# A two-layer S5, Conformer and pooling backbone: modulation in fewer VectorE instructions, x read by place in chunk, and copies moved to ScalarE

## The chip, the core and the metric

The kernel runs on one core of a Trainium2 chip. The metric is the device time of one execution in microseconds (us), the median over runs. The engines in the text are TensorE (PE in the rows), VectorE (DVE), ScalarE (ACT), GpSimd (POOL) and the queue that issues the transfers (SP).

## What is computed

The input is 512 latent tokens of 1024 features and a context of 256 tokens. Two layers follow each other. Layer 0 mixes the tokens with two heads side by side, 32 groups of a bidirectional state-space model and a convolution over 31 tokens; layer 1 takes centred means over windows of 2 to 16 tokens. Both end in an MLP with a squared ReLU. Each norm is followed by a scale and a shift from a projection of c:

```python
n_x = modulate(rms_norm(h, norm_mix_g[i]), sh1, sc1)      # h * (1 + scale) + shift
# layer 0
z = h @ w_in                                              # u | v | gt, 512 each
ya = y_f + flip(y_b) + d_skip * u                         # state-space model, both directions, skip term
ya = gelu(ya);  ya = ya * sigmoid(ya @ w_glu)
vb = silu(layer_norm(conv(v * sigmoid(gt)) + conv_b))
y = concatenate([ya, vb]) @ w_out
# every layer
h = h + g1 * y
h = h + g2 * (relu(modulate(rms_norm(h), sh2, sc2) @ w1) ** 2) @ w2
```

## The kernel before

Features lie on the 128 partitions, in 8 tiles; tokens lie along a row. Matmuls keep fp32 accuracy with three products: each operand is split into a high part, rounded to the fast format fp32r, and the rest, the low part (`split`, L143: a conversion and a subtraction). `mm3` (L147) issues the three products. The matmul operands of a whole stage are the tiles `nh` and `nl`. Weights arrive raw, ScalarE makes the high part and VectorE the low one (`Ring.get`, L223).

**u stage** (`mixer0`, L292, up to about 90 us). The latent x is loaded into `x0` (`load_x`, L239), the position table is added (`add_pos`, L243), and the square root of the mean square is spread to all partitions as R. For each of 8 feature tiles, `u_mod` (L423) multiplies x by R on VectorE, applies scale and shift on ScalarE, and splits the result on VectorE. That ScalarE instruction also changes the order of the tokens: the state-space model cuts the row into chunks of T = 8 tokens, and the matmuls want the tokens by their place k in the chunk, so it reads with a step of 8 elements:

```python
S.activation(t2.rearrange("p (k c) -> p k c", k=T), t.rearrange("p (c k) -> p k c", k=T),
             AF.Identity, bias=ab[:, d, 0, v:v + 1], scale=ab[:, d, 1, v:v + 1])
split(oh, ol, t2, V, el)
```

The same is done for the context (`c_step`, L447), with operands `c`. The products u are collected in six banks, `ux` and `uc`. Sixteen copies, VectorE and ScalarE in turn (`ENG`, key z), bring them into Z; TensorE turns Z over in eight groups of four, and two copies a group, one on each engine, fill U (after L880).

**Steps.** The 32 groups go through the state-space model in 8 steps of four. `step_params` (L581) makes a step's matrices, three steps ahead of `step_main` (L661), where the scan runs on VectorE. One of these matrices, Kt, holds the first taps of the model; its diagonal block has the skip term d_skip. It is put together in `stage` (from L646): for each group two ScalarE copies out of PSUM, a multiply-add of the identity with d_skip, an add of the backward taps; then eight DMAs spread it over the partitions. Between the steps stand the value projections (`vgt`), the convolutions (`conv`) and modulation matmuls, by a list (`FILL`).

**Norm, gelu, gate** (297 to about 320 us). `conv_norm` (L782) makes the conv half of the operands, `nh[4..7]`. `y_out` (L722) turns the model's output over and applies gelu in a scratch tile `ge`; its split fills `nh[0..3]`. `glu_gate` (L824) multiplies with the gate: it adds the high and the low part up again into `yg`, multiplies, and splits once more. Then `out_proj` (L280) runs, first the conv half.

**MLPs and pooling** (from about 345 us). `mlp_norm` (L274) normalises one half of the tokens: VectorE multiplies by R (`norm_mod`, L262), ScalarE applies scale and shift, VectorE converts the high part and subtracts for the low one. `pool_half` (L1072) uses the same `norm_mod`. `up` and `down` stream the weights, three matmuls each.

No order is written by hand: the framework places every instruction by a simulated timeline, so a change in one place moves instructions elsewhere.

Of the kernel before, what the change touches and what calls it, by code (L numbers as in the profile page):

```python
# [17 lines left out]
L = 512  # L18
# [26 lines left out]
    wg="VVVV", gl="VVVV", yl="VVVV", ge="S", z="VS", ul="VVVVVVVV", ucl="VVVVVVVV", pos="VVVVVVVV", ph="V", bb="V", eb="V",  # L45
# [52 lines left out]
def body(tc, I, out, dbg=None):  # L98
# [53 lines left out]
    with tc.tile_pool(name="persist", bufs=1) as P, tc.tile_pool(name="ps", bufs=1, space=PSUM) as PS:  # L152
# [86 lines left out]
        def load_x(t):  # L239
            for d0 in range(0, KT, 2):  # L240
                dma(t[:, d0:d0 + 2], I["xT"][:, d0:d0 + 2])

        def add_pos(e, t, d):  # L243
            hv = t[:, d].rearrange("p (r c) -> p r c", r=8)
            pe = posr[:, d, :, None] if d < 4 else posc[:, d - 4, None, :]
            add(e, hv, hv, pe.to_broadcast([128, 8, 64]))

# [14 lines left out]
        def norm_mod(h, tk, a, b, e):  # L262
            n = tk.stop - tk.start
            R = bcast_rsqrt(sumsq(h, tk), n, D)
            if "G" in ENG[e]:
                rb = tmp("rb", n)
                copy(S, rb, R)
            for d in range(KT):
                t = tmp("tn", n)
                x = E(e, d)  # L270
                mul(x, t, h[:, d, tk], rb if x is G else R)
                yield d, t, a(d), b(d)

        def mlp_norm(h, l, tk):  # L274
            for d, t, a, b in norm_mod(h, tk, lambda d: mod[:, l, 4, d:d + 1], lambda d: mod[:, l, 3, d:d + 1], "tn"):
                S.activation(t, t, AF.Identity, bias=b, scale=a)
                split(nh[:, d, tk], nl[:, d, tk], t, E("nc", d), E("nl", d))
# [14 lines left out]
        def mixer0(P0):  # L292
# [8 lines left out]
            dsk = P0.tile([PH, NG], F32, name="dsk")  # L301
            S2 = P0.tile([128, KT, 32], F32, name="S2")
# [13 lines left out]
            load_x(x0)  # L316
# [53 lines left out]
            def norm_x():  # L370
                for d in range(KT):
                    add_pos(E("pos", d), x0, d)
# [50 lines left out]
            def u_mod(src, R, n, d, v, oh, ol, el):  # L423
                t = tmp("tn", n)
                mul(V, t, src, R)
                t2 = tmp("tm", n)
                S.activation(t2.rearrange("p (k c) -> p k c", k=T), t.rearrange("p (c k) -> p k c", k=T),
                             AF.Identity, bias=ab[:, d, 0, v:v + 1], scale=ab[:, d, 1, v:v + 1])
                split(oh, ol, t2, V, el)
# [128 lines left out]
            def discretise_b(cfr, cfi):  # L558
                def bc(ap):
# [21 lines left out]
            def step_params(st):  # L581
# [67 lines left out]
                for qq in range(GQ):  # L649
# [3 lines left out]
                    q = GQ * st + qq  # L653
                    stt(stage[:, qq, n:n + PH], ident[0:PH, 0:PH], dsk[:, q:q + 1], stage[:, qq, n:n + PH], OP.mult, OP.add)
                    add(V, stage[:, qq, n:n + PH], stage[:, qq, n:n + PH], kb[r, n:n + PH])
# [599 lines left out]
```

## Time and profile before

| | us |
|---|---|
| median of 3 runs | 1141.48 |
| lowest, highest | 1140.08, 1145.19 |
| the profiled execution, time | 1145.11 |
| the profiled execution, span | 1143.3 |
| TensorE busy | 1052.2 (92%) |
| VectorE busy | 843.8 (74%) |
| ScalarE busy | 510.9 (45%) |

The times count from the start of the span. A line `L139` or `L116` is a helper's, so that the names of the tiles tell the place. "Busy" is a share over stages that are bound in different ways; the stretches have to be read one by one.

### The profile page before, as it was taken

How to read it: one execution, taken by the hardware profiler on the slowest of the kernel's cores; microseconds unless marked ns; L12 is line 12 of the kernel's file. 1: busy time of each engine (PE TensorE's matmuls, PEld its weight loads, DVE VectorE, ACT ScalarE, POOL GpSimd, SP SyncE). 2: the span in 40 equal slices, each digit the busy share in tenths (PEclk: the TensorE clock that was granted, in tenths of full speed). 3: DMA queues.
4: the chain of work that ended last, by engine and by line, in shares of the span. 5: the costliest groups of instructions: out<-in, count | busy, mean ns of one | idle time of the engine just before them, and what ended most of it. 6: DMA issues, size and time to landing. Idle time of an engine off the chain costs nothing.

```text
span 1143.3 us, 19141 instructions
## 1 busy us (share of the span) xinstructions
PE 1052.2 (92%) x7342; PEld 894.6 (78%) x7342; DVE 843.8 (74%) x1745; ACT 510.9 (45%) x894; POOL 26.2 (2%) x46
## 2 busy tenths in 40 slices
PE   4888998884898989999999999989979999999996
PEld 3566564543588988888789999989979988888896
DVE  8994988898789789877755669989976543343365
ACT  4553452453545653322324456567545433133153
POOL 1002000000000000000000000000000000000000
PEclk9999998986799999999999999989989999999998
DMA  9442543236245678878754555545536633323352
GB/s 359 133 129 73 160 123 86 65 87 227 68 130 189 194 252 297 289 259 258 255 182 149 178 180 184 167 124 171 168 109 185 186 106 96 92 92 100 103 167 92
DMA packets 63596, 184.84 MB, mean 162 GB/s; under 512 B 8464, under 2 KB 14608, under 8 KB 63376
## 3 DMA queue, kind: packets, MB, share of 16 engines
q1 hardware_dynamic: 63504, 183.61, 50.3%
q8 instruction: 58, 0.95, 0.3%
q14 instruction: 34, 0.28, 0.1%
HBM read 174.96 MB, written 2.10 MB: 155 GB/s over the span
## 4 chain that ended last, share of the span: by engine, by line
PE 52%; DMA 8%; DVE 6%; issue 1%; ACT 1%; POOLq 0%; POOL 0%; DVEq 0%; ACTq 0%
PE ps L148 17%; PE ps L150 17%; PE ps L149 16%; DMA wraw<-in_wadaT 5%; DMA wraw<-in_w 3%; DVE junk L988 2%; DVE wlo L116 2%; ACT whi L139 1%; DVE tn L110 1%; PE ps_r L194 0%; PE ps_p L148 0%; PE ps_p L149 0%; PE ps_p L150 0%; DVE rl L110 0%; PE ps_ms L187 0%
## 5 line engine op out<-in xcount | busy, mean ns | idle before, releaser
L139 ACT ACTIVATE whi<-wraw 128x1024 fp32r<-128x1024 f32 (+1 forms) x232 | 231.5, 1000 | 409.4 <-PE ps L149 267.0
L116 DVE TENSOR_TENSOR wlo<-wraw,whi 128x1024 fp32r<-128x1024 f32 (+1 forms) x232 | 266.2, 1149 | 112.1 <-ACT whi L139 108.4
L148 PE MATMUL ps<-nh,whi 128*128 128x256 f32 (+3 forms) x768 | 248.2, 325 | 10.2 <-DVE nh L141 5.2
L150 PE MATMUL ps<-nh,wlo 128*128 128x256 f32 (+3 forms) x768 | 247.3, 323 | 2.4 <-DVE wlo L116 2.4
L149 PE MATMUL ps<-nl,whi 128*128 128x256 f32 (+3 forms) x768 | 247.4, 323 | 0.0
L150 PE MATMUL ps<-hh,wlo 128*128 128x512 f32 (+3 forms) x768 | 244.1, 318 | 0.4 <-DVE wlo L116 0.4
L148 PE MATMUL ps<-hh,whi 128*128 128x512 f32 (+3 forms) x768 | 243.9, 318 | 0.0
L149 PE MATMUL ps<-hl,whi 128*128 128x512 f32 (+3 forms) x768 | 243.2, 317 | 0.0
L148 PEld LDWEIGHTS ps<-nh,whi 128*128 128x128 f32 x768 | 149.3, 195 | 21.9 <-DVE nh L141 6.3
L150 PEld LDWEIGHTS ps<-nh,wlo 128*128 128x128 f32 x768 | 149.0, 194 | 13.8 <-DVE wlo L116 3.8
L149 PEld LDWEIGHTS ps<-nl,whi 128*128 128x128 f32 x768 | 149.0, 194 | 10.2
L150 PEld LDWEIGHTS ps<-hh,wlo 128*128 128x128 f32 x768 | 144.3, 188 | 12.1 <-DVE wlo L116 1.3
L149 PEld LDWEIGHTS ps<-hl,whi 128*128 128x128 f32 x768 | 144.3, 188 | 10.9
L148 PEld LDWEIGHTS ps<-hh,whi 128*128 128x128 f32 x768 | 144.5, 188 | 9.8
L125 DVE SCALAR_TENSOR_TENSOR h<-ps,mod,h 128x512 f32<-128x512 f32 (+3 forms) x96 | 54.9, 572 | 86.9 <-PE ps L150 86.5
L988 DVE SCALAR_TENSOR_TENSOR junk<-wraw,csil 128x1024 f32<-128x1024 f32 x56 | 68.3, 1220 | 20.4 <-DMA wraw<-in_wadaT 20.3
L116 DVE TENSOR_TENSOR hl<-rl,hh 128x256 fp32r<-128x256 f32 (+3 forms) x96 | 48.4, 511 | 4.8 <-ACT hh L139 3.7
L1014 ACT ACTIVATE rl<-ps 128x256 f32<-128x256 f32 (+3 forms) x96 | 42.0, 437 | 3.4 <-PE ps L149 2.1
L148 PE MATMUL ps_o<-nh,whi 128*128 128x256 f32 x128 | 37.7, 299 | 5.2 <-DVE nh L141 2.7
L149 PE MATMUL ps_o<-nl,whi 128*128 128x256 f32 x128 | 37.5, 294 | 2.5 <-DVE nl L116 2.5
L150 PE MATMUL ps_o<-nh,wlo 128*128 128x256 f32 x128 | 37.4, 298 | 2.1 <-DVE wlo L116 1.9
L348 PE MATMUL ps_ada<-wraw,S 128*32 128x128 f32 x512 | 28.1, 317 | 5.7 <-DMA wraw<-in_wada0b 5.5
(279 smaller groups left out, 1437.1 us busy)
## 6 DMA issues: line engine op xcount, KB each, us to landing
wraw<-in_w SPq DMA_DIRECT2D x192, 512.0 KB, 3.6
wraw<-in_wadaT SPq DMA_DIRECT2D x56, 512.0 KB, 4.6
wraw<-in_wada0b SPq DMA_DIRECT2D x24, 512.0 KB, 4.1
wraw<-in_wout SPq DMA_DIRECT2D x32, 256.0 KB, 2.8
cvt<-vpad SPq DMA_DIRECT2D x64, 67.5 KB, 2.0
wah<-in_wada SPq DMA_DIRECT2D x16, 256.0 KB, 4.6
wraw<-in_wada SPq DMA_DIRECT2D x8, 512.0 KB, 5.3
wraw<-in_win_vg SPq DMA_DIRECT2D x8, 512.0 KB, 4.0
```

The lines of the kernel that those rows point to most:

```text
L110: e.tensor_tensor(o, a, b, op=OP.mult)
L116: e.tensor_tensor(o, a, b, op=OP.subtract)
L125: V.scalar_tensor_tensor(o, a, s, b, op0=op0, op1=op1)
L139: S.activation(o, a, AF.Copy)
L148: PE.matmul(ps, wh, xh, start=first, stop=False)
L149: PE.matmul(ps, wh, xl, start=False, stop=False)
L150: PE.matmul(ps, wl, xh, start=False, stop=last)
L348: PE.matmul(ps[32 * j:32 * j + 32, i * 128:i * 128 + 128], S2[:, kt, :], w[kt], start=kt % 2 == 0, stop=kt % 2 == 1, tile_position=(0, 32 ...
L988: V.scalar_tensor_tensor(junk, w, 1.0, csil, op0=OP.mult, op1=OP.mult, accum_out=r)
L1014: S.activation(t, ps, AF.Relu)
```

## The change

The modulation gets shorter: VectorE multiplies by the scale and by R in one instruction, ScalarE adds the shift and writes the high part directly, and VectorE makes the low part from the same product (`split_shift`); the conversion goes. To do so in the u stage, x and the context come already ordered by place in chunk (xK, ctxT), and the position table is added in that order (`add_pos_k`); the latent stream h is still loaded from xT later. The skip term of a step is one add of a prepared table Dd, behind the four adds of the backward taps. All copies into Z and U run on ScalarE, and so do the high parts of the gelu, the norm and the gate. The gelu output is kept in four tiles of its own, so that the gate needs no adding up. The smaller DMA scratch leaves room in SBUF. What is computed stays.

```diff
@@ ENG
-    ... z="VS", ...
+    ... z="S", ...
@@ body
-        def load_x(t):
+        def load_x(t, src):
             for d0 in range(0, KT, 2):
-                dma(t[:, d0:d0 + 2], I["xT"][:, d0:d0 + 2])
+                dma(t[:, d0:d0 + 2], I[src][:, d0:d0 + 2])
+        def add_pos_k(e, t, d):
+            hv = t[:, d].rearrange("p (k r m) -> p k r m", k=T, r=8)
+            if d < 4:
+                pe = posr[:, d, None, :, None]
+            else:
+                pe = posc[:, d - 4].rearrange("p (m k) -> p k m", k=T)[:, :, None, :]
+            add(e, hv, hv, pe.to_broadcast([128, T, 8, 8]))
-        def norm_mod(h, tk, a, b, e):
+        def norm_scale(h, tk, a, b):
             n = tk.stop - tk.start
             R = bcast_rsqrt(sumsq(h, tk), n, D)
...
             for d in range(KT):
                 t = tmp("tn", n)
-                x = E(e, d)
-                mul(x, t, h[:, d, tk], rb if x is G else R)
-                yield d, t, a(d), b(d)
+                stt(t, h[:, d, tk], a(d), R, OP.mult, OP.mult)
+                yield d, t, b(d)
+        def split_shift(o_h, o_l, t, b):
+            S.activation(o_h, t, AF.Identity, bias=b)
+            stt(o_l, t, b, f(o_h), OP.add, OP.subtract)
         def mlp_norm(h, l, tk):
-            for d, t, a, b in norm_mod(...):
-                S.activation(t, t, AF.Identity, bias=b, scale=a)
-                split(nh[:, d, tk], nl[:, d, tk], t, E("nc", d), E("nl", d))
+            for d, t, b in norm_scale(...):
+                split_shift(nh[:, d, tk], nl[:, d, tk], t, b)
@@ mixer0
+            Dd = P0.tile([PH, NG, PH], F32, name="Dd")
-            load_x(x0)
+            load_x(x0, "xK")
-                    add_pos(E("pos", d), x0, d)
+                    add_pos_k(E("pos", d), x0, d)
@@ u_mod
                 t = tmp("tn", n)
-                mul(V, t, src, R)
-                t2 = tmp("tm", n)
-                S.activation(t2.rearrange("p (k c) -> p k c", k=T), t.rearrange("p (c k) -> p k c", k=T),
-                             AF.Identity, bias=ab[:, d, 0, v:v + 1], scale=ab[:, d, 1, v:v + 1])
-                split(oh, ol, t2, V, el)
+                stt(t, src, ab[:, d, 1, v:v + 1], R, OP.mult, OP.mult)
+                split_shift(oh, ol, t, ab[:, d, 0, v:v + 1])
@@ discretise_b
+                mul(V, Dd, ident[0:PH, None, 0:PH].to_broadcast([PH, NG, PH]), dsk[:, :, None].to_broadcast([PH, NG, PH]))
@@ step_params, for each of the four groups of a step, and after them
-                    q = GQ * st + qq
-                    stt(stage[:, qq, n:n + PH], ident[0:PH, 0:PH], dsk[:, q:q + 1], stage[:, qq, n:n + PH], OP.mult, OP.add)
                     add(V, stage[:, qq, n:n + PH], stage[:, qq, n:n + PH], kb[r, n:n + PH])
+                add(V, stage[:, :, n:n + PH], stage[:, :, n:n + PH], Dd[:, qs])
@@ y_out
-                    t = tmp("ge")
+                    t = P0.tile([128, 512], F32, name="ge", tag="ge", bufs=4)
+                    ges.append(t)
...
-                    split(nh[:, b], nl[:, b], t, V, E("yl", b))
+                    split(nh[:, b], nl[:, b], t, S, E("yl", b))
@@ conv_norm
-                    split(nh[:, 4 + j], nl[:, 4 + j], xn, V, V)
+                    split(nh[:, 4 + j], nl[:, 4 + j], xn, S, V)
@@ glu_gate
-                    y = tmp("yg")
-                    add(V, y, f(nh[:, j]), f(nl[:, j]))
+                    y = ges[j]
                     mul(V, y, y, glu[j])
-                    split(nh[:, j], nl[:, j], y, V, E("gl", j))
+                    split(nh[:, j], nl[:, j], y, S, E("gl", j))
@@ the transposes into U
                 copy(S, us[:, :, NCC:128], pv)
-                copy(V, us[:, :, 0:NCC], pv[:, :, NCH:NJ])
+                copy(S, us[:, :, 0:NCC], pv[:, :, NCH:NJ])
@@ pool_half
-                    S.activation(xp[:, 16 + 16 * x:16 + 16 * x + ns], t, AF.Identity, bias=b, scale=a)
+                    S.activation(xp[:, 16 + 16 * x:16 + 16 * x + ns], t, AF.Identity, bias=b)
@@ layout, kernel
-    X["ctxT"] = a["ctx"][0].T.reshape(KT, 128, LC).transpose(1, 0, 2)
+    X["xK"] = X["xT"].reshape(128, KT, NCH, T).transpose(0, 1, 3, 2).reshape(128, KT, L)
+    X["ctxT"] = a["ctx"][0].T.reshape(KT, 128, NCC, T).transpose(1, 0, 3, 2).reshape(128, KT, LC)
-    nc = _bacc.Bacc("TRN2", target_bir_lowering=False, num_devices=1)
+    nc = _bacc.Bacc("TRN2", target_bir_lowering=False, num_devices=1, dynamic_dma_scratch_size=2048)
```

The order on three places follows. First ScalarE at the end of the u stage (`tm` and `nh` are the modulated tiles of x, `c_...` those of the context, `uc` and `ux` the banks of products that Z is copied from). Before:

```order
L427 ACTIVATE tm<-tn,ab 128x512
L139 ACTIVATE hx<-Cc 64x4x16
L636 ACTIVATE hx<-Cc 64x4x16
L139 ACTIVATE hx<-Cc 64x4x16
L636 ACTIVATE hx<-Cc 64x4x16
L633 ACTIVATE Oi<-Oi 128x4x128
L139 ACTIVATE Z<-uc 32x32x16 x2
L139 ACTIVATE stage<-ps_k 16x112
L139 ACTIVATE Z<-uc 32x32x16
L139 ACTIVATE Z<-ux 64x32x16 x2
L139 ACTIVATE Z<-uc 32x32x16
L139 ACTIVATE Z<-ux 64x32x16 x2
```

and now:

```order
L282 ACTIVATE c_839<-tn,ab 128x256
L282 ACTIVATE nh<-tn,ab 128x512
L139 ACTIVATE hx<-Cc 64x4x16
L646 ACTIVATE hx<-Cc 64x4x16
L139 ACTIVATE hx<-Cc 64x4x16
L646 ACTIVATE hx<-Cc 64x4x16
L643 ACTIVATE Oi<-Oi 128x4x128
L139 ACTIVATE Z<-uc 32x32x16 x8
L139 ACTIVATE Z<-ux 64x32x16 x8
L139 ACTIVATE stage<-ps_k 16x112
L769 ACTIVATE sg<-ps_vg 128x512
L139 ACTIVATE U<-ps_u 128x4x96
```

The sixteen copies into Z stand in one row behind each other, all of uc first, and the `stage` copy that stood among them is behind. On TensorE the same place, the last products of the context (`uc`) and of x (`ux`), was before:

```order
L435 MATMUL uc<-wuh,c_865 128x512
L436 MATMUL uc<-wul,c_865 128x512
L437 MATMUL uc<-wuh,c_865 128x512 x2
L435 MATMUL ux<-wuh,nh 128x512
L436 MATMUL ux<-wul,nh 128x512
L435 MATMUL ux<-wuh,nh 128x512
L436 MATMUL ux<-wul,nh 128x512
L435 MATMUL ux<-wuh,nh 128x512
```

and is now:

```order
L443 MATMUL ux<-wuh,nh 128x512
L444 MATMUL ux<-wul,nh 128x512
L443 MATMUL ux<-wuh,nh 128x512
L444 MATMUL ux<-wul,nh 128x512
L443 MATMUL ux<-wuh,nh 128x512
L444 MATMUL ux<-wul,nh 128x512
L653 MATMUL ps_k<-Or,Bb 16x128
L445 MATMUL uc<-wuh,c_839 128x512 x2
L445 MATMUL ux<-wuh,nl 128x512 x4
```

The low-part products of the context (`x2`) have moved from ahead of the eight products of x with nh to behind them, so uc is complete later.

Second, ScalarE in the norm, gelu and gate (`ln`, `cvt`: the conv half; `ge`, `yx`: the gelu; `glu`: the gate). Before:

```order
L139 ACTIVATE yx<-ps_t 128x4x64 x2
L806 ACTIVATE ln_3022<-cvt,sm 128x512
L807 ACTIVATE cvt<-cvt,sm 128x512
L806 ACTIVATE ln_3029<-cvt,sm 128x512
L806 ACTIVATE ln_3036<-cvt,sm 128x512
L736 ACTIVATE ge<-yx 128x512 x2
L807 ACTIVATE cvt<-cvt,sm 128x512 x3
L738 ACTIVATE ge<-ge,ones 128x512 x2
L742 ACTIVATE ge<-ge 128x512 x2
L139 ACTIVATE whi<-wraw 128x512 x2
L842 ACTIVATE glu<-ps_gl 128x512 x3
L139 ACTIVATE whi<-wraw 128x512 x5
```

and now, where four yx copies, three sigmoids on cvt and two squares of yx stand ahead of this piece:

```order
L819 ACTIVATE cvt<-cvt,sm 128x512
L818 ACTIVATE ln_2982<-cvt,sm 128x512
L750 ACTIVATE ge<-ge,ones 128x512
L819 ACTIVATE cvt<-cvt,sm 128x512
L750 ACTIVATE ge<-ge,ones 128x512
L819 ACTIVATE cvt<-cvt,sm 128x512 x2
L139 ACTIVATE nh<-cvt 128x512
L754 ACTIVATE ge<-ge 128x512
L139 ACTIVATE nh<-cvt 128x512
L754 ACTIVATE ge<-ge 128x512
L139 ACTIVATE nh<-cvt 128x512 x2
L139 ACTIVATE nh<-ge 128x512 x2
```

Six conversions `nh<-` have come in, after or among the affine and gelu passes; before, VectorE made them.

Third, VectorE in the MLP norm of layer 1, first half of the tokens. Before:

```order
L110 TENSOR_TENSOR tn<-h,ps_r 128x256 x6
L141 CAST nh<-tn 128x256 x3
L116 TENSOR_TENSOR nl<-tn,nh 128x256 x2
L141 CAST nh<-tn 128x256
L116 TENSOR_TENSOR nl<-tn,nh 128x256
L110 TENSOR_TENSOR tn<-h,ps_r 128x256
L141 CAST nh<-tn 128x256
L110 TENSOR_TENSOR tn<-h,ps_r 128x256
L141 CAST nh<-tn 128x256
L116 TENSOR_TENSOR nl<-tn,nh 128x256 x2
```

and now:

```order
L125 SCALAR_TENSOR_TENSOR tn<-h,mod,ps_r 128x256 x6
L125 SCALAR_TENSOR_TENSOR nl<-tn,mod,nh 128x256 x5
L125 SCALAR_TENSOR_TENSOR tn<-h,mod,ps_r 128x256
L125 SCALAR_TENSOR_TENSOR nl<-tn,mod,nh 128x256
L125 SCALAR_TENSOR_TENSOR tn<-h,mod,ps_r 128x256
L113 TENSOR_TENSOR sq<-sq 128x248
L125 SCALAR_TENSOR_TENSOR nl<-tn,mod,nh 128x256
L113 TENSOR_TENSOR sq<-sq 128x248
L125 SCALAR_TENSOR_TENSOR nl<-tn,mod,nh 128x256
```

The casts are gone, and the low parts stand directly behind the six multiplies, which are now of the scalar form.

## Rows read from the trace of the kernel before

**Rows 1.** Busy us (instructions) by stretch: TensorE, weight load, VectorE, ScalarE, GpSimd; clock, DMA.

```profile
17.00:88.00 71.00, 60.33 (x404) 42.60 (x405) 68.27 (x258) 38.35 (x64) 5.97 (x3) 0.95 0.50 172
97.00:114.00 17.00, 15.37 (x155) 12.42 (x154) 3.68 (x11) 5.45 (x12) 0.16 (x2) 0.92 0.34 115
114.00:297.00 183.00, 155.26 (x1530) 95.90 (x1530) 160.16 (x350) 82.50 (x211) 7.24 (x14) 0.87 0.43 127
297.00:345.00 48.00, 41.58 (x259) 36.39 (x257) 41.05 (x80) 25.57 (x46) 0.00 (x0) 0.89 0.30 90
345.00:400.00 55.00, 49.44 (x380) 47.56 (x380) 46.95 (x107) 32.79 (x58) 2.13 (x4) 0.97 0.60 192
400.00:1143.00 743.00, 718.39 (x4543) 651.41 (x4541) 503.94 (x898) 313.77 (x485) 4.60 (x6) 0.98 0.54 171
```

**Rows 2.** Groups on VectorE, 0 to 500 us: count, busy us, mean ns, idle before.

```profile
L125 DVE SCALAR_TENSOR_TENSOR h<-ps_o,mod,h 128x256 f32<-128x256 f32 x32 | 15.3, 481 | 2.8 <-PE ps_o L150 2.7
...
L125 DVE SCALAR_TENSOR_TENSOR stage<-ident,dsk,stage 16x16 f32<-16x16 f32 x32 | 7.2, 253 | 2.1 <-ACT stage L139 1.8
...
L110 DVE TENSOR_TENSOR tn<-h,ps_r 128x256 f32<-128x256 f32 x16 | 5.9, 417 | 0.3 <-PE ps_r L194 0.3
...
L113 DVE TENSOR_TENSOR stage<-stage,ps_k 16x16 f32<-16x16 f32 x32 | 5.2, 163 | 4.2 <-ACT stage L139 3.4
...
L113 DVE TENSOR_TENSOR x<-x,sm 128x512 f32<-128x512 f32 x8 | 5.2, 686 | 0.4 <-DMA x<-in_xT 0.3
...
L110 DVE TENSOR_TENSOR vpad<-ps_vg,sg 128x512 f32<-128x512 f32 x4 | 4.4, 1096 | 2.0 <-PE ps_vg L150 2.0
...
L141 DVE CAST nh<-tn 128x256 fp32r<-128x256 f32 x16 | 4.2, 290 | 0.0
...
L141 DVE CAST nh<-tm 128x512 fp32r<-128x512 f32 x8 | 3.4, 424 | 0.2 <-ACT tm L427 0.2
...
L113 DVE TENSOR_TENSOR yg<-nh,nl 128x512 f32<-128x512 f32 x4 | 2.7, 687 | 0.0
...
L141 DVE CAST c<-tm 128x256 fp32r<-128x256 f32 x8 | 2.4, 294 | 0.0
```

**Rows 3.** Groups on ScalarE, 0 to 500 us.

```profile
L427 ACT ACTIVATE tm<-tn,ab 128x512 f32<-128x512 f32 x8 | 10.7, 1336 | 6.6 <-DVE tn L110 4.7 <-DVE ab L122 1.9
...
L807 ACT ACTIVATE cvt<-cvt,sm 128x512 f32<-128x512 f32 x4 | 3.0, 801 | 0.0
...
L139 ACT ACTIVATE wuh<-wu 128x512 fp32r<-128x512 f32 x8 | 5.0, 624 | 0.4 <-DVE wul L116 0.4
```

**Rows 4.** Timeline at the end of the u stage: start, length, engine.

```profile
83.32 0.68 DVE L110 TENSOR_TENSOR tn<-x,scr 128x512 f32<-128x512 f32 x1
...
86.87 0.42 DVE L141 CAST nh<-tm 128x512 fp32r<-128x512 f32 x1
...
88.53 1.28 DVE L141 COPY Z<-uc 32x512 f32<-32x512 f32 x2
...
92.21 0.50 PE L148 MATMUL ps_vg<-nh,whi 128*128 128x512 f32 x1 [0.91 <-ACT Z L139]
```

**Rows 5.** Timeline of the norm, gelu and gate.

```profile
295.77 1.19 ACT L139 ACTIVATE yx<-ps_t 128x256 f32<-128x256 f32 x2 [0.74 <-PE ps_t L727]
...
300.49 0.43 DVE L141 CAST nh<-cvt 128x512 fp32r<-128x512 f32 x1
...
300.97 0.50 PE L148 MATMUL ps_o<-nh,whi 128*128 128x256 f32 x2 [1.30 <-DVE nh L141]
...
310.65 0.76 DVE L141 CAST nh<-ge 128x512 fp32r<-128x512 f32 x2
```

**Rows 6.** Timeline of the layer 1 MLP norm, first half.

```profile
752.36 2.07 DVE L110 TENSOR_TENSOR tn<-h,ps_r 128x256 f32<-128x256 f32 x6
...
754.34 0.69 DVE L141 CAST nh<-tn 128x256 fp32r<-128x256 f32 x3
...
754.68 1.01 PE L148 MATMUL ps<-nh,whi 128*128 128x256 f32 x3 [2.79 <-DVE nh L141]
```

More of the change, by code (lines that the diff above doesn't have):

```diff
@@ L44 @@
 ENG = dict(
-    wg="VVVV", gl="VVVV", yl="VVVV", ge="S", z="VS", ul="VVVVVVVV", ucl="VVVVVVVV", pos="VVVVVVVV", ph="V", bb="V", eb="V",
+    wg="VVVV", gl="VVVV", yl="VVVV", ge="S", z="S", ul="VVVVVVVV", ucl="VVVVVVVV", pos="VVVVVVVV", ph="V", bb="V", eb="V",
     g="VVVVVVVVVVVVVVVVVVVVVVVVVVVVVVVVVVVVVVVVVVVVVVVV", e="VVVVVVVVVVVVVVVVVVVVVVVVVVVVVVVVVVVVVVVVVVVVVVVV", o="VVVVVVVVVVVVVVVVVVVVVVVVVVVVVVVVVVVVVVVVVVVVVVVV",
@@ L260, in sumsq @@
             return list(acc.values())
-        def norm_mod(h, tk, a, b, e):
+        def norm_scale(h, tk, a, b):
             n = tk.stop - tk.start
             R = bcast_rsqrt(sumsq(h, tk), n, D)
-            if "G" in ENG[e]:
-                rb = tmp("rb", n)
-                copy(S, rb, R)
             for d in range(KT):
                 t = tmp("tn", n)
-                x = E(e, d)
-                mul(x, t, h[:, d, tk], rb if x is G else R)
-                yield d, t, a(d), b(d)
+                stt(t, h[:, d, tk], a(d), R, OP.mult, OP.mult)
[3 more added lines that the diff above has]
+            stt(o_l, t, b, f(o_h), OP.add, OP.subtract)
         def mlp_norm(h, l, tk):
-            for d, t, a, b in norm_mod(h, tk, lambda d: mod[:, l, 4, d:d + 1], lambda d: mod[:, l, 3, d:d + 1], "tn"):
-                S.activation(t, t, AF.Identity, bias=b, scale=a)
-                split(nh[:, d, tk], nl[:, d, tk], t, E("nc", d), E("nl", d))
+            for d, t, b in norm_scale(h, tk, lambda d: mod[:, l, 4, d:d + 1], lambda d: mod[:, l, 3, d:d + 1]):
+                split_shift(nh[:, d, tk], nl[:, d, tk], t, b)
         def out_proj(ring, h, d, parts, tk, tags="sc"):
@@ L720, in step_main @@
                              ps[:, 0:ni * 128].rearrange("p (i k h) -> p i k h", i=ni, k=T), AF.Copy)
+            ges = []
             def y_out(bb, ysb):
@@ L934, in fill @@
                         hh.append(htile("h", [128, KT, L]))
-                        load_x(hh[0])
+                        load_x(hh[0], "xT")
                         for d in range(KT):
@@ L1074, in pool_half @@
                 n, ns = tk.stop - tk.start, src.stop - src.start
-                for d, t, a, b in norm_mod(h, src, lambda d: mod[:, 1, 1, d:d + 1], lambda d: mod[:, 1, 0, d:d + 1], "tp"):
+                for d, t, b in norm_scale(h, src, lambda d: mod[:, 1, 1, d:d + 1], lambda d: mod[:, 1, 0, d:d + 1]):
                     gi = d // 2
```

## The prediction

> **What bounds the kernel now.** I read the busy time by stretch first. From 400 us on TensorE is busy 718.39 us of 743 [rows 1]: there the matmuls set the time, and vector work is free unless a matmul waits for it. Before that it is otherwise. From 17 to 88 us VectorE is busy 68.27 us of 71, TensorE 60.33; from 114 to 297 us, the eight state-space steps, VectorE 160.16 us of 183 and TensorE 155.26; ScalarE is never over 60% [rows 1]. The one hole is 97 to 114 us: VectorE has 3.68 us of work in 17, TensorE 15.37, so VectorE time saved just before it buys nothing by itself; only an earlier matmul does. The change takes work from VectorE, partly onto ScalarE. So each part is asked: was VectorE the last to finish there, and is ScalarE now?
>
> Durations are those of the instruction groups [rows 2]; back to back, one instruction overlaps the next by about 0.08 us (two 0.42 us casts took 0.76 [rows 5], three 0.29 us casts 0.69 [rows 6]), which I take off when I add up engine time. A multiply with a per-partition scalar costs 0.064 us more than a plain one: 481 against 417 ns at 256 columns [rows 2].
>
> **Part by part. (1) u stage, Z and U.** Gone from VectorE: 8 casts of 0.344 and 8 of 0.214 us net [rows 2], 4.5 us. Added: 32 scalar forms at 0.064, 2.0 us, and the table Dd, one 512-wide multiply, 0.6 us. The position add of the new x has its table read at a step of eight floats for the four column tiles. No row has that form on VectorE; the bounds are 686 ns as now (a strided read is free) and 1096 ns, the one group that writes at a step of eight floats, vpad [rows 2]. So 0 to 4 x 0.41 = 1.6 us more; I take 0, because these adds begin while x still lands, and keep 1.6 for the range. VectorE gets 0.3 to 1.9 us shorter here.
>
> The ScalarE instruction at L427 reads at that same step and takes 1336 ns; the same function on contiguous data takes 801 [rows 3]. The Trainium skill (Advanced Engine Details and Errata, SBUF Cachelines) says that SBUF is read in 16-byte lines and that an access pattern which meets a new line with every element pays. By that rule the four new table reads pay as well, and the sum below becomes 1134.1 us instead of 1132.5; the two rows on ScalarE agree with it, and no row shows it for a VectorE read.
>
> What counts is when the last tile is ready. Now: multiply at 83.32, ScalarE, then a cast that stands in VectorE's queue until 86.87 and ends at 87.29 [rows 4]. After it the multiply is 0.06 longer, ScalarE needs 0.80, and no cast follows: about 84.9, 2.4 us earlier. Behind it the Z copies: now both engines share 16 and the first value projection starts at 92.21, having waited for them since they began at 88.53 [rows 4]. In the new order ScalarE does the eight uc copies and then the eight ux copies (the first order piece), 0.54 us each net [rows 3], four of which free the first bank: 2.2 us where 3.6 passed. But the last uc products now stand behind the ux high products, some 2 us, which takes back most of this and part of the 2.4. I take **-2.0 us** at 92.21, and the stretch to 114 then moves as a whole: the 8 small U copies cost VectorE nothing now (it is idle) and follow ScalarE's own copies either way. Bounds: -4.5 (nothing taken back) and +2 (all 16 on one engine at 8.7 us, and the strided adds).
>
> **(2) The steps.** The skip term was 32 instructions of 253 ns [rows 2], net 5.5 us; now 8 adds of 16x64, nearest row the 16x16 add of 163 ns [rows 2], net about 0.1 each, 1.0. Two of the four gelu casts lie here, 0.7. VectorE loses 5.2 us. It is the busier engine, but at 160.16/183 = 0.875, and the other eighth is waiting for something else; I credit that share, **-4.5 us**. Bounds 0 and -5.2.
>
> **(3) Norm, gelu, gate (297 to 345).** VectorE loses 10 casts of 0.344 and 4 adds of 0.687 [rows 2], net 5.9 us. But the casts go to ScalarE, which in the new order has, from its first yx copy on, four yx, eight affine or sigmoid passes of 0.80, six gelu passes and six conversions (second order piece). With 0.62 for those without a row of their own [rows 3] that is 8 x 0.80 + 16 x 0.62 - 24 x 0.08 = 14.4 us; from 295.77 [rows 5] it ends at 310.2, where the last cast now ends at 311.4 [rows 5]. The first product of the output projection moves back from 300.97 [rows 5] to about 307, the last operand hardly at all. I take **0**: VectorE gives way and ScalarE takes its place. Bounds -4 and +6.
>
> **(4) MLP norms.** Each of four halves loses 8 casts of 0.29 and has 16 scalar forms. In the two late halves TensorE stands: the multiplies start at 752.36, the casts at 754.34, the first matmul at 754.68 after 2.79 us of waiting [rows 6]. Now the first tile needs one multiply (0.48) and one ScalarE pass (0.6 to 0.8), so the matmul comes 1.0 to 1.2 us sooner. But its fourth matmul needs the low part, which still stands behind six multiplies, 0.4 each now (third order piece): only 0.2 us sooner. Between these I take -0.7 a half, **-1.4 us** (bounds -0.4 and -2.4). In the two early halves (345 to 400 us) VectorE loses 16 x 0.21 - 32 x 0.064 = 1.3 us at a share of 46.95/55 [rows 1], **-1.1 us**. In the pool norm 16 scalar forms add 1.0 us beside a TensorE that is busy 97%: 0; without that cover it would be 1.0.
>
> The loads keep number and size (x0 from another layout, the later h from the old one), and the smaller DMA scratch only makes room in SBUF: 0.
>
> **Sum:** -2.0 - 4.5 + 0 - 1.4 - 1.1 = -9.0 us. The profiled execution took 1145.11 us (its span 1143.3); it would become 1136.1. It stands 3.6 us over the median of the three runs, 1141.48, from which I forecast **1132.5 us**.
>
> **The rivals.** *All of it pays.* If VectorE is the real limit everywhere up to 400 us, count its time alone: 1.9 in the u stage, 8 Z copies at 0.6 (4.8; two took 1.28 [rows 4]), 5.2 in the steps, 5.9 in the gate, 1.3 in the early norms, and the late halves' 1.4: 20.5 us, so 1121. For it: VectorE at 96% in the u stage. Against: the hole at 97 to 114 us and ScalarE's list in (3).
>
> *Little of it pays.* The step loop waits on TensorE and on transfers, whose shares are near VectorE's (155.26 against 160.16 us), and the hole swallows the start: only (4) is left, 1139.
>
> *ScalarE becomes the limit, slower.* The place is the stretch from 295.77. Conversions stand in ScalarE's queue behind gelu passes that wait for VectorE, so the high parts of the conv tiles come late and the output projection starts late. It decides if the last conversion ends after 311.4; each us beyond goes straight into the time. If the whole six us by which the first product is put off reach the end, and (1) and (2) give nothing while (4) is eaten by the strided adds, the time is 1141.5 + 6 = 1148. Against it: ScalarE has 25.57 us of work in these 48 now [rows 1].
>
> **Chances.** Forecast 0.54, all pays 0.16, little pays 0.23, ScalarE slower 0.07. A measurement here tells apart about 0.5%, 5.7 us: faster means under 1135.8. Faster gets the first two cases, 0.70; no change the third, 0.23; slower the last, 0.07. The range for 8 in 10 goes from 1119 (all pays, with the bound -4.5 in (1)) to 1142 (little pays, 1139, and +2 in (1), and one for rounding); outside it lie the slower case and an edge of the first rival.
>
> **What would show it.** Right: the first value projection starts near 90 instead of 92.2 us; VectorE is some 5 us less busy in the steps and the gap between the first value projection and the end of the steps is 4 to 5 us shorter; from there to 345 us nothing is won, with ScalarE's list unbroken; the late norms show a wait of about 1.7 instead of 2.79 us. Wrong: if the gelu and gate stretch gets shorter by several us (VectorE was the limit there too), if the steps keep their length with a wait on a transfer or TensorE in the place of VectorE, or if the start is later because of the adds.

## Result and profile after

| | before | after |
|---|---|---|
| median, us | 1143.34 (1140.08 to 1147.23, 4 runs) | 1130.43 (1128.84 to 1132.73, 4 runs) |
| profiled execution, time (span), us | 1145.11 (1143.3) | 1131.62 (1129.7) |

The ratio is 0.9886, 95% interval 0.9856 to 0.9915: 13 us faster, to 1130.43, with 1132.5 forecast. The total came out; the terms did not. Start of the same instruction in the two timelines, in us:

| | before | after | shift |
|---|---|---|---|
| first of the last four products into `ux` | 90.10 | 88.51 | -1.6 |
| first value projection, `ps_vg` | 92.21 | 93.19 | +1.0 |
| first transpose of Z, `ps_u` | 100.27 | 105.79 | +5.5 |
| first state product, `ps_v` (the steps begin) | 114.56 | 120.02 | +5.5 |
| last copy into `ysb` (the steps end) | 294.66 | 288.58 | -6.1 |
| first product of the output projection, `ps_o` | 300.97 | 300.18 | -0.8 |
| last `ps_o` | 371.39 | 365.00 | -6.4 |
| 1153rd product of the MLPs, of 4608 (half of the first layer's) | 606.83 | 592.74 | -14.1 |
| last product of the MLPs | 1132.11 | 1118.56 | -13.6 |

So the start lost 5.5 us, the steps won 11.5, the stretch behind them nothing (0.3), the first half of the first layer's MLP 7.7, all the rest nothing (0.5 lost). These are single executions: in the run with the new norm alone (below), which up to 348 us issues the instructions of the kernel before in the same order on every engine, the first `ps_v` came at 118.02 and the last `ysb` at 296.53, 3.5 and 1.9 us later. A shift under some 3 us in such a table tells nothing by itself. The busy times of the same stretches, columns as in [rows 1]:

```profile
17.00:88.00 71.00, 60.55 (x414) 45.26 (x414) 68.37 (x241) 29.22 (x63) 8.21 (x6) 0.93 0.49 170
97.00:114.00 17.00, 15.61 (x141) 12.50 (x140) 1.28 (x2) 9.08 (x25) 0.16 (x2) 0.97 0.21 68
114.00:297.00 183.00, 155.93 (x1562) 96.63 (x1562) 157.88 (x328) 91.42 (x226) 9.71 (x14) 0.91 0.44 133
297.00:345.00 48.00, 43.91 (x296) 40.51 (x297) 39.78 (x76) 28.77 (x53) 1.16 (x1) 0.93 0.36 105
345.00:400.00 55.00, 50.10 (x398) 48.16 (x396) 49.70 (x98) 33.08 (x62) 0.97 (x3) 1.00 0.68 216
```

VectorE is as busy as before from 17 to 88 us (68.37 against 68.27): 17 instructions fewer, but longer ones. These are VectorE's groups by shape that answer to [rows 2]:

```profile
L113 DVE TENSOR_TENSOR x<-x,sm 128x512 f32<-128x512 f32 x8 | 6.8, 887 | 0.4 <-DMA x<-in_xK 0.4
L125 DVE SCALAR_TENSOR_TENSOR tn<-h,mod,ps_r 128x256 f32<-128x256 f32 x16 | 6.9, 475 | 0.3 <-PE ps_r L194 0.3
L125 DVE SCALAR_TENSOR_TENSOR c<-tn,ab,c 128x256 fp32r<-128x256 f32 x8 | 5.4, 684 | 0.0
```

The position adds rose from 686 to 887 ns. The scalar form at 256 columns takes 475 ns (481 was used), yet the `c` group has a mean of 684. The timeline of the end of the u stage, answering to [rows 4], shows why, and what it did. Before:

```profile
84.14 8.44 POOL L110 TENSOR_TENSOR hx<-sm,sel 128x1024 f32<-128x1024 f32 x2 [57.66 <-DVE tn L110]
84.73 1.29 DVE L110 TENSOR_TENSOR hx<-PO,Cc 128x512 f32<-128x512 f32 x2
87.01 0.73 PE L437 MATMUL uc<-wuh,c 128*128 128x512 f32 x2 [0.94 <-DVE c L116]
87.81 0.69 DVE L116 TENSOR_TENSOR nl<-tm,nh 128x512 fp32r<-128x512 f32 x1
```

and after:

```profile
81.53 4.71 POOL L110 TENSOR_TENSOR hx<-sm,sel 128x1024 f32<-128x1024 f32 x2 [52.23 <-DVE tn L125]
82.33 2.14 DVE L125 SCALAR_TENSOR_TENSOR c<-tn,ab,c 128x256 fp32r<-128x256 f32 x1
84.39 3.00 DVE L110 TENSOR_TENSOR hx<-PO,Cc 128x512 f32<-128x512 f32 x2
86.74 0.73 PE L445 MATMUL uc<-wuh,c 128*128 128x512 f32 x2
87.72 0.74 DVE L125 SCALAR_TENSOR_TENSOR nl<-tn,ab,nh 128x512 fp32r<-128x512 f32 x1
90.10 0.63 ACT L643 ACTIVATE Oi<-Oi 128x512 f32<-128x512 f32 x1 [7.24 <-DVE Oi L113]
90.75 2.99 ACT L139 ACTIVATE Z<-uc 32x512 f32<-32x512 f32 x5
93.19 0.79 PE L148 MATMUL ps_vg<-nh,whi 128*128 128x512 f32 x1 [1.68 <-ACT Z L139]
```

While GpSimd made its two products, VectorE needed 2.14 us for an instruction of 0.48, and 3.00 for a pair that took 1.29 in the kernel before; there VectorE kept its pace, and the same two GpSimd products took 8.44 us instead of 4.71. The stretching adds up to 3.4 us. VectorE's `Oi` ended 3.4 us later than before (at 90.06 instead of 86.62), ScalarE stood behind its own negation of `Oi` for 7.24 us, and the Z copies, now ScalarE's alone, stood behind that in its queue: they start at 90.75, and at 88.53 before [rows 4]. The last products into `uc` did not come later, against what stands with the order of TensorE above: they start at 86.74, before at 87.01.

In the steps I compare the stretch from the first `ps_v` to the last `ysb` copy, before and after:

```profile
114.56:294.66 180.10, 152.36 (x1515) 93.92 (x1514) 157.72 (x344) 80.90 (x208) 7.24 (x14) 0.87 0.42 126
```
```profile
120.02:288.58 168.56, 146.31 (x1495) 89.91 (x1494) 152.65 (x316) 81.42 (x207) 9.71 (x14) 0.91 0.44 129
```

Busy time by the mean granted clock of the stretch is an estimate of the work at full speed: 152.36 x 0.87 = 132.6 us and 146.31 x 0.91 = 133.1, nearly the same. Of the 11.5 us, 5.4 are then idle TensorE (27.7 to 22.3), and the other 6 or so went at the lower of its clock's two levels (1.2 instead of 2.4 GHz). VectorE has 5.1 us less work, as forecast. That looked like the skip term paying twice. The experiments say otherwise.

### The profile page after: what moved, and what is told of

Same layout as the page of the kernel before. It is cut to its first block, busy times and chain, and to the rows that moved or that the text cites. A ratio compares the mean times of both kernels' runs of the same rounds, so it can differ in the third digit from the quotient of the medians.

```text
span 1129.7 us, 19052 instructions
## 1 busy us (share of the span) xinstructions
PE 1044.0 (92%) x7342; PEld 891.5 (79%) x7342; DVE 828.2 (73%) x1642; ACT 512.3 (45%) x922; POOL 27.1 (2%) x46
## 4 chain that ended last, share of the span: by engine, by line
PE 51%; DMA 7%; DVE 7%; issue 1%; ACT 1%; POOLq 0%; POOL 0%; DVEq 0%; ACTq 0%
PE ps L150 17%; PE ps L148 16%; PE ps L149 16%; DMA wraw<-in_wadaT 4%; DMA wraw<-in_w 3%; DVE junk L999 2%; DVE wlo L116 2%; ACT whi L139 1%; DVE tn L125 1%; PE ps_r L194 0%; DVE hl L116 0%; PE ps_p L150 0%; PE ps_p L148 0%; PE ps_p L149 0%; DVE nl L125 0%
## 5 line engine op out<-in xcount | busy, mean ns | idle before, releaser
L359 PE MATMUL ps_ada<-wraw,S 128*32 128x128 f32 x512 | 25.0, 313 | 14.8 <-DMA wraw<-in_wada0b 14.6
```

The source lines that it names most:

```text
L359: PE.matmul(ps[32 * j:32 * j + 32, i * 128:i * 128 + 128], S2[:, kt, :], w[kt], start=kt % 2 == 0, stop=kt % 2 == 1, tile_position=(0, 32 ...
```

## The experiments

Each kernel ran beside the kernel before on the same chip; ratios are to that kernel, with 95% intervals, and 0.1% is 1.14 us. The changed kernel is at 0.9886.

### One part undone, or done alone

**The skip term as it was**, in the changed kernel:

```
-                add(V, stage[:, :, n:n + PH], stage[:, :, n:n + PH], Dd[:, qs])
+                    stt(stage[:, qq, n:n + PH], ident[0:PH, 0:PH], dsk[:, GQ * st + qq:...], ..., OP.mult, OP.add)
```

> The changed kernel with one part undone: the skip term is again four scalar multiply-adds of 16x16 a step, and the table Dd is gone. Theory A (my prediction's term 2): VectorE loses 4.5 us of shorter steps, so the total is +3 to +4.5 us above the changed kernel and the steps lengthen by as much. Theory B (from the traces: the stretch from the first to the last ps_v product shortened by 18.7 us, and TensorE's wait for the Kt transfer behind the stage tile fell from 10.4 to 1.5 us): the short chain from stage to Kt transfer is what the steps waited for, the wait for Kt returns to 8 to 10 us and the total is +8 to +13 us. Theory C (the steps became shorter for another reason, the casts that left VectorE or the new order of the loads): total within 2 us, the wait for Kt stays at 1.5 to 3 us.

Ratio 0.9883 (0.9855 to 0.9912): no difference. In its trace the steps are 4.8 us longer (173.4), but they begin 2.6 us sooner, the stretch behind them is 2.1 us shorter, and the last `ps_o` starts at 365.18 against 365.00. TensorE's wait for the Kt transfer (10.4 us in the kernel before) does not come back. The lines are the waits in the steps: in all, how often, the longest. First the kernel before, then the changed one, then this run:

```profile
PE ps_y L715 <- DMA Kt<-stage: 10.4, 2, 7.5
PE ps_ada L348 <- DMA wraw<-in_wada0b: 4.4, 3, 2.5
```
```profile
PE ps_y L724 <- DMA Kt<-stage: 1.5, 2, 1.0
PE ps_ada L359 <- DMA wraw<-in_wada0b: 12.0, 7, 3.3
```
```profile
PE ps_y L724 <- DMA Kt<-stage: 1.9, 2, 1.3
```

Theory C holds: the skip term is not what removed that wait, and no part of the 13 us can be seen to come from it. In the changed kernel TensorE waits longer than before for loads (`in_wada0b`, 12.0 us instead of 4.4).

**The norm before the MLPs**: the old one put back into the changed kernel, and the new one alone put into the kernel before. The diff is of the first:

```
-                stt(t, h[:, d, tk], a(d), R, OP.mult, OP.mult)
-                split_shift(nh[:, d, tk], nl[:, d, tk], t, b)
+                mul(V, t, h[:, d, tk], R)
+                S.activation(t, t, AF.Identity, bias=b, scale=a(d))
+                split(nh[:, d, tk], nl[:, d, tk], t, V, V)
```

> The changed kernel with the old norm before the MLPs in all four halves: multiply by the scale, ScalarE's affine pass, cast to the high part on VectorE, subtraction. The order of work up to the first of these norms (about 345 us) is the same. Theory A (my prediction's term 4): +1.1 us in the two early halves, +1.4 us in the two late ones, total +2.5 us. Theory B (from the traces: 6 us were won between 365 and 405 us, where VectorE was at 100% and TensorE, waiting, ran at a lower granted clock): +6 us in the early halves and 0 to +1 in the late ones, total +6 to +7.5 us; VectorE at 95 to 100% there again, TensorE's granted clock in 375 to 405 us at 0.85 to 0.9. Theory C (those 6 us came from the tail being early, not from the norm): total within 1 us.

> The kernel before with the new norm before the MLPs alone (scale folded into the multiply, ScalarE's biased pass writes the high part, the low part by a fused subtraction), in all four halves; the order of work ahead of the first half is that of the kernel before. Theory A (my prediction's term 4): -2.5 us. Theory B (from the two traces, which won 6 us between 365 and 405 us): -6 to -7.5 us. Theory G (from undoing the norm in the changed kernel, which cost 0.3% in the ratios): -3 to -5 us, of it no more than 1 us in the two late halves, and the rest in the second early half, where VectorE is busy 100% now.

Undone: 0.9915 (0.9887 to 0.9943), 3.3 us worse, with overlapping intervals, so that its three theories can't be told apart (its profiled execution, 1145.71 us, was 10 us above its median, so its times in the trace are not used). Alone: 0.9952 (0.9933 to 0.9971), **5.5 us won**, 3.3 to 7.7. Nearest is theory G, a little exceeded; the interval also holds the 6 to 7.5 us of theory B, and not the 2.5 of theory A. In its trace the distance from the first to the 1153rd MLP product went from 235.3 to 228.8 us, and from there to the last one it stayed at 525.3: all of it lies in the early halves. The other traces bear this out, with some spread: in the eleven that have the new norm this first distance is 226.5 to 231.4 us, in the kernel before with the copies on ScalarE, which has the old one, 231.3. The 50 us from 2 us ahead of the first MLP product, in the kernel before, with the new norm alone, and in the changed kernel:

```profile
369.51:419.51 50.00, 44.94 (x343) 44.08 (x342) 40.86 (x87) 27.25 (x49) 0.74 (x1) 0.93 0.67 215
```
```profile
371.20:421.20 50.00, 47.20 (x385) 46.33 (x385) 44.35 (x87) 30.01 (x53) 0.75 (x1) 1.00 0.74 239
```
```profile
363.12:413.12 50.00, 48.26 (x392) 47.26 (x392) 45.55 (x89) 30.64 (x54) 0.74 (x1) 1.00 0.77 248
```

Before, TensorE idles 5.1 us here, nearly all of it for converted weights (`whi`), and the granted clock is 0.93. With the new norm it idles 2.8 or 1.7 us, at 1.00. That less work on VectorE brings the weights sooner fits the queue of the loads, whose longest waits in these 50 us (here in the kernel before) are all for VectorE; it was not tested by itself.

```profile
SPq L220 <- DVE rl L110: 19.8, 6, 4.7
SPq L220 <- DVE wlo L116: 6.3, 4, 2.4
```

**The high parts on VectorE**, ten conversions, the gelu output still kept:

```
-                    split(nh[:, b], nl[:, b], t, S, E("yl", b))
+                    split(nh[:, b], nl[:, b], t, V, E("yl", b))
```

(the same in `conv_norm` and `glu_gate`).

> The changed kernel with the ten high parts of the gelu, conv-norm and gate tiles cast on VectorE again; the gelu tiles are still kept, so the four adds stay away. Theory A (my prediction's term 3: VectorE gives way and ScalarE takes its place, so moving the casts was worth nothing between 289 and 365 us): total within 1 us of the changed kernel, the two high gelu parts in the steps included. Theory B (VectorE was the limit there): each cast costs its 0.34 us again, total +2 to +3.5 us. Theory C (ScalarE is the limit there now): the casts back on VectorE are a gain, total -2 to -4 us, the first output projection product 3 to 6 us sooner after the last ysb copy than now.

Ratio 0.9903 (0.9871 to 0.9934), not to be told from the changed kernel. The first product of the output projection, here and in the changed kernel:

```profile
293.17 0.48 PE L148 MATMUL ps_o<-nh,whi 128*128 128x256 f32 x2 [1.52 <-DVE nh L141]
```
```profile
300.18 0.58 PE L148 MATMUL ps_o<-nh,whi 128*128 128x256 f32 x1 [5.88 <-ACT nh L139]
```

On ScalarE the first product is 7.0 us later (5.1 counted from the last `ysb`), and yet the last `ps_o` starts at 365.00, on VectorE at 365.01. This fits theory A. But ScalarE is not shown to be the limit in VectorE's place: from 300 to 340 us TensorE is busy 39.2 us of 40 in the changed kernel and 37.9 here.

**The position table in x's order**, so that the adds read it contiguously (the later adds into `h` read it with a step):

```
-                pe = posc[:, d - 4].rearrange("p (m k) -> p k m", k=T)[:, :, None, :]
+                pe = posc[:, d - 4].rearrange("p (k m) -> p k m", k=T)[:, :, None, :]
```

> The changed kernel with the position table stored in x's new order, so that the four adds of the column tiles read it contiguously; the later adds into h, between 270 and 345 us, read it with a step instead. The order of all instructions on all engines is the same as in the changed kernel. Theory A (the strided reads cost what the trace shows, 1.07 against 0.69 us, and the adds lie on the path to the first norm): the first sum of squares is ready 1.2 to 1.6 us sooner, the adds take 0.69 us each, and the total falls by 0.5 to 1.5 us. Theory B (what is won there is lost behind a load or a full queue later): the adds are shorter, the total is the same within 0.5 us. The strided adds into h cost VectorE 1.5 us where ScalarE sets the pace: nothing by either.

Ratio 0.9902 (0.9875 to 0.993): nothing to be told. VectorE's two groups, by shape:

```profile
L113 DVE TENSOR_TENSOR x<-x,sm 128x512 f32<-128x512 f32 x8 | 5.2, 685 | 1.1 <-DMA x<-in_xK 1.1
```
```profile
L113 DVE TENSOR_TENSOR h<-h,sm 128x512 f32<-128x512 f32 x8 | 6.7, 878 | 0.0
```

The price moved with the strided read, from x (887 to 685 ns) to h (675 to 878): 0.4 us for each strided add. The sum of squares was ready at 17.7 us instead of 18.7, although x landed 0.6 us later, and the first `ps_v` still started at 119.96 (120.02), as theory B has it.

### The copies into Z and U

**All copies shared again; Z alone; U alone; and the copies on ScalarE in the kernel before:**

```
-    ge="S", z="S",          (Z)
+    ge="S", z="VS",
-                copy(S, us[:, :, 0:NCC], pv[:, :, NCH:NJ])          (U)
+                copy(V, us[:, :, 0:NCC], pv[:, :, NCH:NJ])
```

> The changed kernel with one part undone: the Z copies alternate between VectorE and ScalarE again, and the small U copies are VectorE's again. Everything else of the change stays. Theory A (my prediction's term 1, -2.0 us for ScalarE alone): giving the copies back makes the start of the steps later or leaves it, first state-space product at 120 us or up to 2 us after it, total 0 to +2 us above the changed kernel. Theory B (from the two traces: ScalarE alone is the reason that the first step began 5.5 us later, because its queue stood behind a negation of Oi and then copied 16 banks alone): the first ps_u transpose comes at about 100 to 102 us instead of 105.8, the steps begin 3 to 5.5 us sooner, total -3 to -5.5 us. Theory C (what the start wins is lost in the steps, which wait for loads): the steps begin sooner as in B and end at the same place, total within 1 us.

> The changed kernel with the Z copies alone shared between VectorE and ScalarE again; the small U copies stay on ScalarE. Theory A (my prediction): 0 to +2 us. Theory D (VectorE's time before the first step is what counts: 8 copies of 0.6 us plus what stands behind them): +4 to +6 us, all of it lost before 125 us. Theory E (order: with the copies shared the planner puts the loads and the Kt transfers into SP's queue in another order, as it did in the run where Z and U were both shared): +10 to +16 us, less than 5 of them lost before 125 us and the rest in the steps, with TensorE's wait for the Kt transfer at 5 us or more.

> The changed kernel with the eight small U copies alone back on VectorE; the Z copies stay on ScalarE. The order of the loads on SP stays the same. Theory A (my prediction: VectorE is idle there, these copies cost nothing either way): total within 1 us of the changed kernel. Theory D (the copies' own time on ScalarE counts): ScalarE's list before the first step gets shorter by 8 x 0.3 us, the steps begin 1 to 2 us sooner, total -1 to -2 us.

> The kernel before with one part of the change done: all Z copies and the small U copies on ScalarE. Theory A (my prediction's term 1): VectorE's share gone, ScalarE's longer, total within 2 us of the kernel before. Theory D (undoing this part in the changed kernel took away all of its gain, 14 us, so this part carries it by itself): total -9 to -14 us against the kernel before. Theory E (the gain needs this part together with the others, because it comes from the order that the planner finds and the places of the loads in SP's queue, and not from the copies' own time): total -4 to +4 us here, and the place where the time goes is not at the copies (88 to 120 us) but in the steps behind, where TensorE waits for Kt and for loads.

| | ratio | interval |
|---|---|---|
| changed, Z and U shared | 1.0010 | 0.9987 to 1.0033 |
| changed, Z shared | 1.0044 | 1.0025 to 1.0062 |
| changed, U on VectorE | 0.9908 | 0.9881 to 0.9935 |
| before, Z and U on ScalarE | 1.0001 | 0.9985 to 1.0016 |

Here theories A, B, C and D of the first runs all fell. Sharing the Z copies takes the whole gain away (14 and 18 us), and yet giving them to ScalarE in the kernel before gains nothing. A fixed price of the copies would be the same in both. Of the theories on record theory E, the order, comes nearest, though two of its marks were missed: the 18 us lie above its 10 to 16, and the wait for Kt with Z alone shared is 4.5 us, not 5 or more. (With U alone on VectorE nothing can be told from the changed kernel, which fits A.) With Z alone shared the loss grew at 120 to 140 us, where the granted clock was 0.50 throughout, the lower level, against 0.95 in the changed kernel:

```profile
120.00:140.00 20.00, 17.18 (x114) 12.46 (x115) 14.79 (x28) 6.68 (x15) 0.20 (x3) 0.50 0.71 210
```

It begins at the copies (the run with Z and U shared):

```profile
94.48 1.07 ACT L139 ACTIVATE Z<-uc 32x512 f32<-32x512 f32 x2
95.61 2.39 ACT L139 ACTIVATE Z<-ux 64x512 f32<-64x512 f32 x4
98.72 1.19 ACT L139 ACTIVATE Z<-uc 32x512 f32<-32x512 f32 x2 [0.73 <-DVE Z L141]
99.36 0.80 PE L148 MATMUL ps_vg<-nh,whi 128*128 128x512 f32 x1 [5.23 <-ACT Z L139]
```

The value projection takes over a `uc` bank, and the last `uc` copies stand behind the `ux` ones: TensorE waits 5.23 us in either run (1.68 in the changed kernel). So I freed the `uc` banks first.

**Z divided by bank**, `uc` on ScalarE, `ux` on VectorE:

```
-                        copy(E("z", k2), Z[0:64, ...
+                        copy(V, Z[0:64, ...
```

> The changed kernel with the Z copies divided by bank and no longer by turns: the eight from the uc banks on ScalarE, the eight from the ux banks on VectorE; the small U copies stay on ScalarE. In both runs with the copies by turns, the last two uc copies of each engine stood behind its four ux copies, and TensorE's first value projection, which takes over a uc bank, waited 5.2 us for them; its granted clock then was 0.5 to 0.66 until 102 us. Here ScalarE frees the uc banks first, as in the changed kernel. Theory F (that wait and the clock behind it started the 14 us): the first ps_vg waits 2 us at most, TensorE's granted clock is back at 1.00 by 108 us, and the total is within 3 us of the changed kernel, although VectorE again does half the copies. Theory D (VectorE's time for the copies is what costs): +4 to +6 us. Theory E (the order of loads and of VectorE's queue in the steps, which differ from the changed kernel's here too): the first ps_vg is early as in F, the total is nevertheless +5 us or more, and it is lost between 120 and 300 us at a single wait of over 4 us in VectorE's or TensorE's queue.

Ratio 1.0026 (1.0004 to 1.0047), still 16 us above the changed kernel, though the first `ps_vg` starts at 94.63 after a wait of 1.3 us and the first `ps_v` only 1.8 us later than there. F fell, E held: the loss is in the steps (184.6 us long, against 168.6), and on VectorE it has one large place:

```profile
226.81 1.09 DVE L110 TENSOR_TENSOR vpad<-ps_vg,sg 128x512 f32<-128x512 f32 x1 [9.22 <-PE ps_vg L150]
227.75 0.54 DVE L110 TENSOR_TENSOR rr<-ps_v,Er 128x384 f32<-128x384 f32 x1
```

The gate of the fourth value chunk (`vpad`) stands in VectorE's queue ahead of the next scan (`rr`). Here the last 15 of the chunk's matmuls come behind products of the convolutions on TensorE (`ps_cv`), in the changed kernel the last three, and there the same multiply waits 0.32 us. In the run with Z and U shared it waits 6.76 us, in the kernel before with the copies on ScalarE 8.58. It isn't the only place: with Z alone shared it waits 0.88, and that run is the slowest. So I moved that chunk.

**The fourth value projection earlier in the fill list**, in the run with Z divided by bank and, as control, in the changed kernel:

```
-FILL = ("v1", "", "c0 v2 a2", "c1 c2 v3", "a3 y", "c3", ...)
+FILL = ("v1", "", "c0 v2 a2", "v3 c1 c2", "a3 y", "c3", ...)
```

> The kernel with the Z copies divided by bank, and one entry of the fill list changed: the fourth value projection is entered ahead of the convolutions of chunks one and two, not behind them. Its products then all stand ahead of the state products that they stood behind, and the vpad multiply that reads them stands a step earlier in VectorE's queue. In the run with the copies divided by bank that multiply held VectorE's queue for 9.22 us at 217 to 227 us, with the next scan behind it; TensorE then waited for the Kt and hx transfers of that scan, and its granted clock was 0.5 to 0.9 from 258 to 300 us. Theory H (that one wait is most of the loss): no wait for ps_vg over 3 us on VectorE between 120 and 300 us, and the total falls by 8 to 14 us against that run, to 1133 to 1139 us. Theory I (the steps lose the same time at whatever wait comes next, because the copies on VectorE cost their own time or the loads are late): the wait for ps_vg is gone, others take its place, and the total falls by less than 4 us.

> The changed kernel with the same entry of the fill list changed, the control to the run beside it: here the vpad multiply of the fourth chunk waited 0.32 us only, so there is nothing of that kind to win. Theory H: within 3 us of the changed kernel (1127 to 1134 us), and so near the other run of this pair, where ScalarE has half the Z copies only. Theory I: any change over 3 us here would come from other places in the order, and would show how much the order by itself moves the time, with no instruction added or taken away.

Ratios 0.9942 (0.992 to 0.9963) and 0.9938 (0.9915 to 0.9961). The run with divided copies falls by 9.6 us, as theory H said, and the same multiply no longer waits:

```profile
193.33 1.10 DVE L110 TENSOR_TENSOR vpad<-ps_vg,sg 128x512 f32<-128x512 f32 x1
```

The steps of the two runs with divided copies, without and with the edit:

```profile
121.84:306.46 184.62, 154.23 (x1510) 97.85 (x1509) 153.61 (x318) 81.56 (x209) 6.01 (x14) 0.86 0.41 122
```
```profile
119.83:295.18 175.35, 153.76 (x1493) 93.52 (x1496) 153.52 (x320) 82.90 (x209) 6.13 (x14) 0.89 0.42 126
```

VectorE's work is the same, 153.6 and 153.5 us; TensorE idles 21.6 instead of 30.4 us. The control missed H: it is 5.9 us slower than the changed kernel (the intervals just touch), with no instruction added or taken away. So the edit moves more than that one wait, and the 9.6 us are not shown to be the wait's alone. And with this list no difference is seen (0.9942, 0.9938) whether VectorE has half the Z copies or none.

## Why the prediction was right in the total and wrong in its terms

That the total came out was luck. In the two profiled executions the gain was 13.5 us, against 9.0 in the sum. The start came 7.5 us worse than forecast, the steps 7 us better and the MLPs with their norms nearly 5 us better (-7.2 against -2.5), misses that partly cancel. Of the 4.5 us left over, the base of the forecast took some: 1141.48 lies 1.9 us under the median of the four runs.

**(1) u stage, Z and U: -2.0 forecast, +5.5 measured at the first state product, outside its bounds.** Three steps failed. "I take 0, because these adds begin while x still lands": the strided adds cost 0.4 us each, nearly the upper bound of 1.6 us in all, and the adds did not hide under the load. The rule that spoke against this choice (the Trainium skill, Advanced Engine Details and Errata, SBUF Cachelines) was right about the reads; what it added to the sum, 1.6 us, was lost again before the steps. "Four of which free the first bank: 2.2 us": the copies took that long (93.19 less 90.75), but I read ScalarE's queue only from the copies on and not the negation of `Oi` in front of them, which waited 7.24 us. "The stretch to 114 then moves as a whole": it did not, since the transposes of Z now stand behind 45 value products instead of 35. The last tile's high part did come sooner, at 82.2 us instead of 87.3; but its low part, which the last products into `ux` need as well, stands behind the stretched multiplies and starts at 87.72, before at 87.81. That copies on VectorE need not cost anything that can be seen is shown by the last two runs, in their order.

**(2) Steps: -4.5 forecast, -11.5 measured in the profile, and 0 in the total from the skip term.** VectorE lost the 5 us as counted. With the skip term put back VectorE had 6.3 us more work in the steps (158.95 against 152.65), and in that one execution they were 4.8 us longer, not far from the share I credited; yet nothing of it reached the last `ps_o`. The failing step is the one behind "I credit that share": the 4.5 us went into the sum as if the stretches before and behind stayed as they are. The other 7 us I did not foresee. What can be read is that TensorE's wait for Kt went (10.4 to 1.5 us) and that for loads grew. The fourth `vpad` multiply is not the place here: it waits 0.03 us in the kernel before and 0.32 in the changed one. Why the steps got shorter stays open; the runs show only that the order can move them that much.

**(3) Norm, gelu, gate: 0 forecast, 0 measured** (-6.1 us at the last `ysb`, -6.4 at the last `ps_o`). The shape came out, the first product back by 7.0 us and the last not at all. That ScalarE takes VectorE's place as the limit is not shown, since the conversions can be on either engine and TensorE is busy nearly all the time from 300 to 340 us.

**(4) MLP norms: -2.5 forecast, -5.5 measured alone.** Both of its terms were off. Late halves, -1.4 forecast, 0 measured: the first matmul waits 1.4 us instead of 2.79 [rows 6], as worked out, but the fourth then waits 1.1 for its low part:

```profile
739.37 0.71 PE L148 MATMUL ps<-nh,whi 128*128 128x256 f32 x3 [1.41 <-ACT nh L282]
741.18 0.58 PE L149 MATMUL ps<-nl,whi 128*128 128x256 f32 x1 [1.10 <-DVE nl L125]
```

I had seen both and took the middle; the later one decides. Early halves, -1.1 forecast, -6.5 measured alone and -7.7 in the changed kernel. I scaled VectorE's saved time by its share; but VectorE also makes the low parts of the weights, and what TensorE waited there cost clock as well: the granted clock is 0.93 over the 50 us in the kernel before, and 1.00 with the new norm.

**The rivals.** "All of it pays" needed VectorE to be the limit everywhere; (2) and (3) speak against it. "Little of it pays" was nearer in its reasons: of the two parts put alone into the kernel before, the copies and the norm, only the norm (4) shows a gain. "ScalarE becomes the limit" was right about the late first operand and wrong about the end.

**What is shown and what is not.** The norm carries about 5.5 of the 13 us (3.3 to 7.7), and its trace shows them in the stretch that was edited. Nothing else carries a share of its own that these runs can show, and one entry of the fill list gives or takes 6 to 10 us. The other 7 us are thus of the size of what the order alone moves. That they are the order and nothing else is argued from this, not shown part by part: the new modulation of the u stage, the kept gelu tiles and the smaller DMA scratch were not run alone. No run was faster than the changed kernel by more than the intervals.

## What to carry to other kernels

Where a planner lays out in-order queues, an edit's price is the work it adds plus the new places of everything else: look in the new order for the instruction that stands ahead of the critical one on its engine and waits for a late producer. Before crediting an edit with the gain, move something that adds no work; if that shifts the time as much, the gain may belong to the order. A share of busy time is no exchange rate for saved time; ask for the one wait that ends later.

## What the runs showed of the hardware that was not expected

- A two-input fp32 add on VectorE with one operand at a step of eight floats took 1.09 us for 512 elements (eight adds, four of them strided, with a mean of 887 ns), against 0.69 contiguous.
- VectorE's instructions stretched beside GpSimd's two-input multiply: 2.14 us instead of 0.48, and 3.00 for two of 0.69, one place in each of GpSimd's two instructions (81.53 to 86.24 us). The Trainium skill (SBUF — State Buffer, SBUF: two separate sides) says that VectorE, when it reads two SBUF inputs, and GpSimd share a pair of ports under a lock, and that the loser waits for the whole instruction. The trace agrees: the 3.00 us end 1.2 us, about the two multiplies' own time, behind GpSimd's end. In the kernel before it was the other way round: VectorE kept its pace (1.29 us for the same pair), and GpSimd's two multiplies took 8.44 us instead of 4.71.
